# Half of a feed-forward product by seven block products instead of eight, issued as a written stream

## The chip, the cores and the metric

The kernel runs on one core of a Trainium2 chip. The metric is the device time of one execution in microseconds; the time given is the median of several runs, and one execution more is taken with the profiler.

## The reference

One residual block over 256 tokens of width 2048: a retention branch and a latent-attention branch, merged by gates, and then a feed-forward block. The change touches the feed-forward block alone:

```python
def _rmsnorm(x, g):
    x32 = x.astype(jnp.float32)
    y = x32 * lax.rsqrt(jnp.mean(x32 * x32, axis=-1, keepdims=True) + EPS)
    return (y * g.astype(jnp.float32)).astype(x.dtype)

def reference(...):
    h = x
    for l in range(DEPTH):                      # DEPTH = 1
        u = _rmsnorm(h, norm_mix_g[l])
        h = h + _mixer(u, ...)                  # the two branches and w_out
        z = _rmsnorm(h, norm_mlp_g[l]) @ w_up[l]          # (256, 2048) @ (2048, 8192)
        h = h + jnp.square(jax.nn.relu(z)) @ w_down[l]    # (256, 8192) @ (8192, 2048)
    return _rmsnorm(h, norm_f_g)
```

All data is float32.

## The kernel before

**Arithmetic.** Each float32 operand is split in two parts of the type fp32r: `hi` is a cast on ScalarE, `lo` is the rest, by a subtraction on VectorE (`split`, line 214, and `weights`, line 146, which also loads the weight tile with a DMA from SP's queue). A product then takes three matmuls: hi by hi, hi by lo and lo by hi. Activations are kept as `Pair` tiles, whose hi and lo lie side by side for each block of 128 channels, channels on partitions and tokens along the free axis.

**Units.** `t_unit` (line 170) makes one tile of 128 output columns for all 256 tokens: the stationary operand is a 128x128 block of weights. `t_pass1` (line 157) runs w_hi against x_hi and x_lo together, 16 matmuls of 512 columns; `t_pass2` (line 162) runs w_lo against x_hi, 16 of 256. The two halves of the PSUM tile `z` are then added (`join`, line 204: a copy on ScalarE and a sum on VectorE). Weights come in half units of 512 KB. `n_tile` (line 196) is the other form: blocks of x are stationary, 512 columns of weights move, and the result has tokens on partitions.

**Feed-forward.** After the output projection (four column chunks `c`, tile `wo`, from line 770), `mlp_turn` (line 757) transposes the normalized rows on TensorE and splits them into `hT`. The first feed-forward product is the loop over `FT` = 64 units (lines 792 to 800), each followed by a squared ReLU on VectorE into `hid`, which stays in SBUF. The second product (lines 819 to 832) goes over the 64 blocks of `hid`: each is split into `dh` and `dl`, and `down` (line 807) runs 24 matmuls of 512 columns into eight PSUM tiles `dn`, which take all eight banks. The end (`finish`, `normalize`) scales, adds the residual `hn` and normalizes.

**Order.** The program is written in loops; a scheduler with a modelled timeline fixes each engine's order and the slots of the tiles. Engines work through their own lists in order and wait for each other through semaphores. Where the order matters, single instructions are marked `keep_in_program_order`. Tiles come from pools: `wp` holds weights (5 raw, 4 hi, 4 lo tiles of 4 KB a partition), `act` six large tiles, `pmm` and `pat` four PSUM banks each. Only ScalarE and VectorE evict PSUM; GpSimd works on the position angles at the start (lines 296 to 304), on a few small powers, and on the final gain (line 847).

Of the kernel before, what the change touches and what calls it, by code (L numbers as in the profile page):

```python
# [27 lines left out]
CHUNK = 64  # L28
DFF = 8192
FT = DFF // P  # L30
EPS = 1e-6
QK_SCALE = float(192.0 ** -0.5)
LOWEST = -3.4e38
# [55 lines left out]
def block_kernel(ctx: ExitStack, tc: tile.TileContext, A):  # L89
    nc = tc.nc  # L90
    V, SC, G, PE = nc.vector, nc.scalar, nc.gpsimd, nc.tensor
# [3 lines left out]
    cp = ctx.enter_context(tc.tile_pool(name="cp", bufs=1))  # L95
# [4 lines left out]
    def big(name, dt=F32, shape=(P, KT, S)):  # L100
        return act.tile(list(shape), dt, tag="act16", name=name)
# [31 lines left out]
    def mmps(name):  # L133
        return pmm.tile([P, 512], F32, tag="mm", name=name)
# [4 lines left out]
    uid = [0]  # L139
# [15 lines left out]
    HK = KT // 2  # L155
# [40 lines left out]
    def n_tile(out, w, x, t, k0, nk, start, stop):  # L196
# [4 lines left out]
        for k in range(nk):  # L201
            PE.matmul(out, x.hi(k0 + k, ts), w[1][:, k], start=False, stop=stop and k == nk - 1)

    def join(out, ps):
        t = sm.tile([P, S], F32, tag="join", bufs=2, name="join")
        SC.copy(t, ps[:, S:])
        V.tensor_tensor(out=out, in0=ps[:, :S], in1=t, op=ALU.add)  # L207

    def joined(ps):
        t = sm.tile([P, S], F32, tag="val", bufs=2, name="val")  # L210
        join(t, ps)
        return t

    def split(hi, lo, val, scale=None):
        if scale is None:
            SC.copy(hi, val)  # L216
            V.tensor_tensor(out=lo, in0=val, in1=hi.bitcast(F32), op=ALU.subtract)
# [12 lines left out]
    warm = cp.tile([P, 1], F32, name="warm")  # L230
    SC.activation(warm, halfpi, AF.Copy)

    cold = cp.tile([P, 512], BF16, name="cold")
# [5 lines left out]
    rctx = ExitStack()  # L239
    rope_pool = rctx.enter_context(tc.tile_pool(name="rope", bufs=2))  # L240
    ictx = ExitStack()
    ip = ictx.enter_context(tc.tile_pool(name="ip", bufs=1))

# [8 lines left out]
    x = Pair("x")  # L252
# [97 lines left out]
    rxb = cp.tile([P, S], F32, name="rxb")  # L350
    V.tensor_copy(rxb, pb[:, :S])

    tabs = []
# [1 line left out]
    def table(j):  # L355
        ang, kk = angs[j]
        sgn = vec[:, V_INV + 2 + j : V_INV + 3 + j]
        own = ip if j == 0 else cp
        cos = own.tile([P, S], F32, name=f"cos{j}")
        sin = own.tile([P, S], F32, name=f"sin{j}")  # L360
# [157 lines left out]

    with ExitStack() as mctx:
        cc = big("cc", F32R, shape=(P, 2 * LT, 2, S))  # L520
        kpe = cp.tile([P, S], F32, name="kpe")
        lp = ExitStack()
        lpool = lp.enter_context(tc.tile_pool(name="lp", bufs=1))

# [230 lines left out]
    hT = Pair("hT")  # L755

    def mlp_turn(c):
        for jj in range(2):
            pT = atps(f"ht{c}{jj}")
            for j in range(2):  # L760
                kt = 4 * c + 2 * jj + j
                for t in range(2):
                    o = j * S + t * P
                    PE.transpose(pT[:, o : o + P], hn[:, t, kt * P : (kt + 1) * P], ident)
                g = vec[:, V_MLP + kt : V_MLP + kt + 1]
                split(hT.hi(kt), hT.lo(kt), pT[:, j * S : (j + 1) * S], scale=g)
    hp = ctx.enter_context(tc.tile_pool(name="hp", bufs=1))
    ssh = cp.tile([P, 2, 4], F32, name="ssh")
# [22 lines left out]
    hid.append(hp.tile([P, KT, S], F32, name="hid3"))  # L791
    for i in range(FT):
        if i < 2:
            pz = up[i]
            t_half(pz, A["w_up"][i], hT, 1)
        else:
            pz = mmps(f"z{i}")
# [5 lines left out]
    ssf = cp.tile([P, 2, 68], F32, name="ssf")  # L803
    rf = cp.tile([P, 2], F32, name="rf")
    LAST = 2

    def down(i, t, c, w, hs):
        (hi, lo), (dh, dl) = w, hs
        ts = slice(t * P, (t + 1) * P)
        ws = slice(c % 2 * 512, c % 2 * 512 + 512)  # L810
        out = pd[t][c]
        end = i == FT - 1
        mm = tc.keep_in_program_order if i >= FT - LAST else (lambda ins: ins)
        mm(PE.matmul(out, dh[:, ts], hi[:, ws], start=i == 0, stop=False))  # L814
        mm(PE.matmul(out, dh[:, ts], lo[:, ws], start=False, stop=False))  # L815
        mm(PE.matmul(out, dl[:, ts], hi[:, ws], start=False, stop=end))  # L816

    tail = []
    for i in range(FT):
        dh = hp.tile([P, S], F32R, tag="dh", bufs=3, name=f"dh{i}")  # L820
        dl = hp.tile([P, S], F32R, tag="dl", bufs=3, name=f"dl{i}")
        split(dh, dl, hid[i // KT][:, i % KT])
        ws = []
        for half in range(2):
            w = weights(A["w_down"][i][:, half * 1024 : (half + 1) * 1024], [P, 1024])
            ws.append(w)
            if i < FT - LAST:
                for t in range(2):
                    for c in (2 * half, 2 * half + 1):
                        down(i, t, c, w, (dh, dl))  # L830
        if i >= FT - LAST:
            tail.append((i, ws, (dh, dl)))
# [7 lines left out]
    def finish(t, c, lo, hi, n):  # L840
        h = hn[:, t, c * 512 + lo : c * 512 + hi]
        ps = pd[t][c][:, lo:hi]
        V.scalar_tensor_tensor(h, in0=ps, scalar=rh2[:, t : t + 1], in1=h, op0=ALU.mult, op1=ALU.add)
        junk = hp.tile([P, 512], F32, tag="junk", bufs=2, name=f"junk{t}{n}")
# [32 lines left out]
def _t_units(w):  # L877
    k, n = w.shape
    return np.ascontiguousarray(w.reshape(k // P, P, n // P, P).transpose(2, 1, 0, 3))


def _n_units(w):
    k, n = w.shape
    u = w.reshape(k // 512, 4, P, n // 512, 512).transpose(3, 0, 2, 1, 4)
    return np.ascontiguousarray(u.reshape(-1, P, 4, 512))


def _cols(v):
# [57 lines left out]
```

## Time and profile before

| | |
|---|---|
| median of 3 runs | 1631.68 us (1631.11 to 1632.01) |
| the profiled execution | 1632.22 us, its span 1630.4 us |
| granted TensorE clock | 0.998 |
| first feed-forward product | 915.5 to 1272.7 us from the start |
| second feed-forward product | 1272.7 to 1620.6 us (last matmul's start) |
| weights of 512 KB, issue to landing | 4.2 us median |

The profile is one execution. Its page gives each engine's busy time and the chain of work that ended last, followed back from the end; further views give groups of instructions by line, by tile, in order of time, and the busy time in stretches. In a row of the timeline stand the start in us, the time in us, the engine, the line of the kernel, the operation, the tiles (out<-in), the shape and how many instructions were merged. TensorE's matmuls are pipelined, so the duration of one (0.39 us) is longer than the distance from one to the next.

### The profile page before, as it was taken

Reading aid. Unit: us, or ns where it says so; the run is one execution under the profiler, and the core shown is the slowest. Engines: PE = TensorE matmul, PEld = TensorE weight load, DVE = VectorE, ACT = ScalarE, POOL = GpSimd, SP = SyncE. Lnnn points to the kernel's source line nnn. Section 1 sums busy time; section 2 is a strip of 40 time slices with the busy share of each in tenths; the row PEclk is TensorE's granted clock in tenths of the full one; section 3 lists DMA queues with packets and bytes.
Section 4 is the critical chain, followed back from the end, with each engine's and each line's share of the span. In section 5 each row is a group of like instructions: output and inputs, shape, how many; then the busy total and the mean of one; then the engine's idle time right before and its main releaser. Section 6 shows DMA issues by size and latency. Waiting matters only on the chain.

```text
span 1630.4 us, 23041 instructions
## 1 busy us (share of the span) xinstructions
PE 1614.9 (99%) x8782; PEld 1398.8 (86%) x8782; DVE 996.2 (61%) x1491; ACT 809.7 (50%) x1249; POOL 49.5 (3%) x62
## 2 busy tenths in 40 slices
PE   8999999999999999999999999999999999999997
PEld 6888888888889889888888888888888888888886
DVE  7974588655556658666765555555555555555555
ACT  6544555544445556765545544444444444444444
POOL 7100000000000000000000000000000000000001
PEclk9999999999999999999999999999999999999999
DMA  8665544555556554325575555555555655555553
GB/s 306 200 233 193 187 156 166 169 192 186 190 170 203 190 191 146 125 94 176 186 246 187 174 193 188 192 189 186 191 192 184 223 194 192 193 193 195 192 194 112
DMA packets 84480, 304.46 MB, mean 187 GB/s; under 512 B 9360, under 2 KB 9488, under 8 KB 83600
## 3 DMA queue, kind: packets, MB, share of 16 engines
q1 hardware_dynamic: 84368, 302.98, 55.3%
q8 instruction: 69, 1.13, 0.3%
q14 instruction: 43, 0.35, 0.1%
HBM read 300.84 MB, written 2.10 MB: 186 GB/s over the span
## 4 chain that ended last, share of the span: by engine, by line
PE 97%; DVE 1%; issue 0%; DMA 0%; ACT 0%; POOL 0%; SPq 0%; DVEq 0%; POOLq 0%; ACTq 0%
PE z L159 14%; PE z L163 8%; PE dn L816 7%; PE dn L814 7%; PE dn L815 7%; PE rg L159 4%; PE yr L159 4%; PE gr L159 4%; PE gm L159 4%; PE mo L159 4%; PE qk L159 2%; PE gr L163 2%; PE yr L163 2%; PE gm L163 2%; PE rg L163 2%; PE mo L163 2%
## 5 line engine op out<-in xcount | busy, mean ns | idle before, releaser
L152 DVE TENSOR_TENSOR lo<-raw,hi 128x1024 fp32r<-128x1024 f32 (+2 forms) x562 | 666.0, 1204 | 521.6 <-ACT hi L151 248.3
L151 ACT CAST hi<-raw 128x1024 fp32r<-128x1024 f32 (+2 forms) x562 | 580.8, 1035 | 536.9 <-PE z L159 135.2
L159 PE MATMUL z<-hT,hi 128*128 128x512 f32 x1024 | 245.5, 391 | 0.0
L159 PEld LDWEIGHTS z<-hT,hi 128*128 128x128 f32 x1024 | 188.0, 188 | 36.1
L815 PE MATMUL dn<-lo,dh 128*128 128x512 f32 x512 | 199.2, 389 | 0.0
L816 PE MATMUL dn<-hi,dl 128*128 128x512 f32 x512 | 199.2, 389 | 0.0
L814 PE MATMUL dn<-hi,dh 128*128 128x512 f32 x512 | 198.9, 389 | 0.0
L163 PEld LDWEIGHTS z<-hT,lo 128*128 128x128 f32 x1024 | 131.6, 191 | 5.1
L163 PE MATMUL z<-hT,lo 128*128 128x256 f32 x1024 | 133.1, 283 | 0.0
L815 PEld LDWEIGHTS dn<-lo,dh 128*128 128x128 f32 x512 | 96.1, 188 | 20.1
L816 PEld LDWEIGHTS dn<-hi,dl 128*128 128x128 f32 x512 | 96.1, 188 | 19.9
L814 PEld LDWEIGHTS dn<-hi,dh 128*128 128x128 f32 x512 | 96.1, 188 | 19.8
L216 ACT CAST dh<-hid 128x256 fp32r<-128x256 f32 x64 | 26.0, 407 | 89.3 <-PE dn L815 89.3
L159 PE MATMUL mo<-my,hi 128*128 128x512 f32 x256 | 65.5, 396 | 0.4 <-DVE val L207 0.4
L159 PE MATMUL rg<-x,hi 128*128 128x512 f32 x256 | 64.0, 395 | 0.0
L159 PE MATMUL yr<-ry,hi 128*128 128x512 f32 x256 | 61.4, 391 | 0.0
L159 PE MATMUL gr<-x,hi 128*128 128x512 f32 x256 | 61.3, 391 | 0.0
L159 PE MATMUL gm<-x,hi 128*128 128x512 f32 x256 | 61.1, 391 | 0.0
L159 PEld LDWEIGHTS gm<-x,hi 128*128 128x128 f32 x256 | 47.0, 188 | 9.1
L159 PEld LDWEIGHTS gr<-x,hi 128*128 128x128 f32 x256 | 47.0, 188 | 9.0
L159 PEld LDWEIGHTS yr<-ry,hi 128*128 128x128 f32 x256 | 46.9, 188 | 9.0
L159 PEld LDWEIGHTS rg<-x,hi 128*128 128x128 f32 x256 | 46.2, 188 | 8.6
(271 smaller groups left out, 2239.1 us busy)
## 6 DMA issues: line engine op xcount, KB each, us to landing
raw<-w_up SPq DMA_DIRECT2D x128, 512.0 KB, 4.2
raw<-w_down SPq DMA_DIRECT2D x128, 512.0 KB, 4.3
raw<-w_rv SPq DMA_DIRECT2D x32, 512.0 KB, 4.5
raw<-w_rg SPq DMA_DIRECT2D x32, 512.0 KB, 4.5
raw<-w_gret SPq DMA_DIRECT2D x32, 512.0 KB, 4.3
raw<-w_ret_o SPq DMA_DIRECT2D x32, 512.0 KB, 4.6
raw<-w_gmla SPq DMA_DIRECT2D x32, 512.0 KB, 4.4
raw<-w_out SPq DMA_DIRECT2D x32, 512.0 KB, 3.7
```

The costliest lines, as they stand in the source:

```text
L151: SC.copy(hi, raw)
L152: V.tensor_tensor(out=lo, in0=raw, in1=hi.bitcast(F32), op=ALU.subtract)
L159: PE.matmul(out, w[0][:, k], x.both(k0 + k), start=start and k == 0, stop=False)
L163: PE.matmul(out[:, :S], w[1][:, k], x.hi(k0 + k), start=False, stop=stop and k == n - 1)
L216: SC.copy(hi, val)
L814: mm(PE.matmul(out, dh[:, ts], hi[:, ws], start=i == 0, stop=False))
L815: mm(PE.matmul(out, dh[:, ts], lo[:, ws], start=False, stop=False))
L816: mm(PE.matmul(out, dl[:, ts], hi[:, ws], start=False, stop=end))
```

## The change

The weights of the first feed-forward product are divided. The first 4096 columns are computed in 4 passes (`u`) of 1024 columns, each of 8 steps (`j`) of 256 input channels. A step takes x as 2x2 blocks (128 channels by 128 tokens) and w as 2x2 blocks (128 channels by 512 columns) and adds seven block products to seven PSUM tiles, where the plain form has eight. Four of the seven use sums of weight blocks, which are made for every step: two blocks on GpSimd (`fa`), two on VectorE (`fb`). The sums of x blocks (`Combos.make`) are made once, on VectorE. At the end of a pass `s_end` combines the seven tiles to four result blocks, in part on GpSimd; they have tokens on partitions and are transposed on TensorE (`turn`). The other 4096 columns are computed in 32 plain units (`Unit`), in halves.

Steps (four weight parts each) and units (two parts each) are put in one list, three units at the front, two at the back, and mostly one unit behind each step. A loop under `manual_schedule` issues, for each part, the loads seven parts ahead, the splits four ahead, then the part's matmuls; all five engines keep this order. The halves of a unit are added on GpSimd. The squared ReLU moves to ScalarE (Relu, Square). `hid` is written to DRAM from SP's queue and read back in the second product by GpSimd's queue, two blocks at a time, the plain units' blocks first. `hn` is parked in DRAM meanwhile. Some small tiles move to a pool that closes earlier. (`evict` below is a method of `Unit`.)

```diff
+SU = 4
+SJ = KT // 2
+ST = SU * 1024 // P
+EARLY, LATE = 3, 2
+AHEAD = 4
+PAIRED = 6
+MAKE = 1, 2 * EARLY + 18
+SUMS = (4, 7, 10), (0, 1, 2)
...
+    PRODUCTS = ((3, 0, 0), (4, 0, 1), (2, 1, 0), (5, 1, 1), (6, 2, 0), (1, 2, 1), (7, 3, 0))
+
+    class Combos:
...
+        def make(self, c):
+            if c % 2 == 0:
+                self.t.append(big(f"{self.name}{c // 2}", F32R, (P, KT // 4, 2, 4, P)))
+            x, q = wtile("raw", [P, 2, 2, 2, P]), wtile("raw", [P, 2, 4, P])
+            hi, lo = self.pair.span(4 * c, 4)
+            xs = x.rearrange("p j k t n -> p (j k) (t n)")
+            V.tensor_tensor(out=xs, in0=hi.bitcast(F32), in1=lo.bitcast(F32), op=ALU.add)
...
+            V.tensor_tensor(out=a2, in0=a11, in1=a12, op=ALU.subtract)
+            V.tensor_tensor(out=a5, in0=a11, in1=a21, op=ALU.subtract)
+            yield
+            V.tensor_tensor(out=a6, in0=a2, in1=a21, op=ALU.subtract)
+            V.tensor_tensor(out=a4, in0=a6, in1=a22, op=ALU.add)
+            yield
+            o = self.t[-1][:, c % 2 * 2 : c % 2 * 2 + 2]
+            split(o[:, :, 0], o[:, :, 1], q)
...
+    class Step:
...
+        def load(self, part):
+            if part:
+                return
+            self.rb = wtile("raw", [P, 2, 512])
+            self.ra = zp.tile([P, 2, 512], F32, tag="sraw", bufs=2, name=f"sraw{uid[0]}")
+            nc.sync.dma_start(self.ra, self.src[:, :2])
+            nc.sync.dma_start(self.rb, self.src[:, 2:])
+            self.fa, self.fb = (forms[:, 2 * (self.j % 2) + i] for i in range(2))
+            G.tensor_tensor(
+                out=self.fa, in0=self.rb[:, 1:].to_broadcast([P, 2, 512]), in1=self.ra, op=ALU.add
+            )
+
+        def prep(self, part):
+            r = (self.ra, self.fa, self.fb, self.rb[:, :1])[part]
...
+            split(hi, lo, r)
+            self.ws[part] = hi, lo
+            if part == 0:
+                V.tensor_tensor(out=self.fb[:, 0], in0=self.fa[:, 0], in1=self.ra[:, 1], op=ALU.add)
+                V.tensor_tensor(out=self.fb[:, 1], in0=self.fb[:, 0], in1=self.rb[:, 0], op=ALU.add)
+
+        def mm(self, part):
...
+            if part == 1:
+                self.between()
+            hi, lo = self.ws.pop(part)
+            first, last = self.j == 0, self.j == SJ - 1
+            for f, i, o in PRODUCTS:
+                if i == part:
+                    ah, al = self.x.get(f, self.j)
+                    q = self.qs[f]
+                    PE.matmul(q, ah, hi[:, o], start=first, stop=False)
+                    PE.matmul(q, al, hi[:, o], start=False, stop=False)
+                    PE.matmul(q, ah, lo[:, o], start=False, stop=last)
+            if part == 3 and last:
+                self.end()
+
+    def s_end(qs, out, tmp):
...
+        SC.copy(t3, qs[3])
+        tt(V, e, qs[6], t3)
+        SC.copy(q5, qs[5])
+        tt(V, f, qs[2], e, ALU.subtract)
+        SC.copy(c12, qs[1])
+        tt(V, c21, qs[4], f)
+        SC.copy(c22, qs[7])
+        tt(G, c11, q5, f)
+        yield
+        tt(G, e, e, q5, ALU.subtract)
+        yield
+        tt(G, c12, c12, e)
+        yield
+        tt(G, c22, c22, t3)
+        yield
...
+        if c in (1, 2):
+            for _ in hc.make(c - 1):
+                pass
...
-    up = [mmps(f"z{i}") for i in range(2)]
-    for i in range(2):
-        t_half(up[i], A["w_up"][i], hT, 0)
-        if i == 0:
-            mlp_turn(3)
-    hid = [big(f"hid{i}") for i in range(3)]
...
-            t_unit(pz, A["w_up"][i], hT)
-        z = joined(pz)
-        V.scalar_tensor_tensor(hid[i // KT][:, i % KT], in0=z, scalar=0.0, in1=z, op0=ALU.max, op1=ALU.mult)
+    hid = [hidd.tile([P, 2, S], F32, name=f"hid{i}") for i in range(FT // 2)]
+    forms = big("forms", shape=(P, 4, 2, 512))
...
+    def store(pair, n, t):
+        SC.activation(t, t, AF.Square)
+        later.append([3, lambda: nc.sync.dma_start(hid[pair][:, n : n + t.shape[1]], t)])
...
+        def evict(self):
+            pair, n = divmod(ST + self.i, 2)
+            t = zp.tile([P, 2, S], F32, tag="hs", bufs=4, name=f"hs{pair}{n}")
+            SC.copy(t, self.ps.rearrange("p (j n) -> p j n", j=2))
+            G.tensor_tensor(out=t[:, 0], in0=t[:, 0], in1=t[:, 1], op=ALU.add)
+
+            def rest():
+                SC.activation(t[:, :1], t[:, :1], AF.Relu)
+                store(pair, n, t[:, :1])
+
+            later.append([2, rest])
...
+    with tc.manual_schedule(engines=MANUAL):
+        for n, (it, h) in enumerate(parts):
+            ahead = AHEAD if n else 2
+            while loaded < min(len(parts), n + ahead + 3):
+                parts[loaded][0].load(parts[loaded][1])
+                loaded += 1
+            while prepped < min(len(parts), n + ahead + 1):
+                parts[prepped][0].prep(parts[prepped][1])
+                prepped += 1
+            it.mm(h)
+            if n == 0:
+                mlp_turn(3)
+                keep = hidd.tile([P, 2, D], F32, name="hnkeep")
+                SC.dma_start(keep, hn)
+                zo = big("zo", shape=(P, 2, 4, 512))
+            elif n in MAKE:
+                making = hc.make(2 + MAKE.index(n))
+            if n < 2 * EARLY or n % 2 == 0:
+                next(making, None)
+            for entry in list(later):
+                entry[0] -= 1
+                if entry[0] < 0:
+                    later.remove(entry)
+                    entry[1]()
...
+    hn = big("hn2", shape=(P, 2, D))
+    nc.sync.dma_start(hn, keep)
...
-    for i in range(FT):
+    for n, i in enumerate((*range(ST, FT), *range(ST))):
+        if n % 2 == 0:
+            hl = hp.tile([P, 2, S], F32, tag="hl", bufs=3, name=f"hl{i}")
+            G.dma_start(hl, hid[i // 2])
...
-        split(dh, dl, hid[i // KT][:, i % KT])
+        split(dh, dl, hl[:, i % 2])
```

More of the change, by code (lines that the diff above doesn't have):

```diff
@@ L30 @@
 FT = DFF // P
+SU = 4
[6 more added lines that the diff above has]
+SUMS = (4, 7, 10), (0, 1, 2)
+MANUAL = {getattr(mybir.EngineType, n) for n in ('Activation', 'DVE', 'PE', 'SP', 'Pool')}
+SSF = 68
 EPS = 1e-6
@@ L202, in n_tile, with __init__, get @@
             PE.matmul(out, x.hi(k0 + k, ts), w[1][:, k], start=False, stop=stop and k == nk - 1)
+    PRODUCTS = ((3, 0, 0), (4, 0, 1), (2, 1, 0), (5, 1, 1), (6, 2, 0), (1, 2, 1), (7, 3, 0))
+    class Combos:
+        FORM = {2: 0, 5: 1, 6: 2, 4: 3}
+        RAW = {1: (1, 0), 3: (0, 1), 7: (1, 1)}
+        def __init__(self, name, pair):
+            self.name, self.pair, self.t = name, pair, []
+        def make(self, c):
[5 more added lines that the diff above has]
+            V.tensor_tensor(out=xs, in0=hi.bitcast(F32), in1=lo.bitcast(F32), op=ALU.add)
+            a11, a12, a21, a22 = (x[:, :, k, t] for t in range(2) for k in range(2))
+            a2, a5, a6, a4 = (q[:, :, f] for f in range(4))
+            yield
[7 more added lines that the diff above has]
+            split(o[:, :, 0], o[:, :, 1], q)
+        def get(self, f, j):
+            if f in self.RAW:
+                k, t = self.RAW[f]
+                ts = slice(t * P, (t + 1) * P)
+                return self.pair.hi(2 * j + k, ts), self.pair.lo(2 * j + k, ts)
+            o = self.t[j // 4][:, j % 4]
+            return o[:, 0, self.FORM[f]], o[:, 1, self.FORM[f]]
@@ new lines, in block_kernel, with __init__ @@
+    class Step:
+        def __init__(self, qs, src, x, j, between, end):
+            self.qs, self.src, self.x, self.j, self.between, self.end = qs, src, x, j, between, end
+            self.ws = {}
+        def load(self, part):
[11 more added lines that the diff above has]
+            r = (self.ra, self.fa, self.fb, self.rb[:, :1])[part]
+            if part:
+                n = r.shape[1]
+                hi, lo = (
+                    zp.tile([P, n, 512], F32R, tag=f"{kind}{n}", bufs=3 * n - 2, name=f"{kind}{uid[0]}{part}")
+                    for kind in ("shi", "slo")
+                )
+            else:
+                hi, lo = (wtile(kind, [P, 2, 512]) for kind in ("hi", "lo"))
+            split(hi, lo, r)
[4 more added lines that the diff above has]
+        def mm(self, part):
+            if part == 0 and self.j == 0:
+                self.qs.update({f: (mmps if f in (3, 4, 2, 5) else atps)(f"zs{uid[0]}{f}") for f in (3, 4, 2, 5, 6, 1, 7)})
+            if part == 1:
[11 more added lines that the diff above has]
+                self.end()
@@ new lines, in s_end, with tt @@
+    def s_end(qs, out, tmp):
+        t3, e, f, q5 = (tmp[:, i] for i in range(4))
+        c11, c12, c21, c22 = (out[:, t, c] for t in range(2) for c in range(2))
+        def tt(eng, o, a, b, op=ALU.add):
+            eng.tensor_tensor(out=o, in0=a, in1=b, op=op)
+        SC.copy(t3, qs[3])
[12 more added lines that the diff above has]
+        tt(G, c22, c22, t3)
+        yield
@@ L231, in block_kernel @@
     SC.activation(warm, halfpi, AF.Copy)
[L233 removed]
+    rctx = ExitStack()
+    rope_pool = rctx.enter_context(tc.tile_pool(name="rope", bufs=2))
+    cold = rope_pool.tile([P, 512], BF16, tag="cold", bufs=1, name="cold")
     V.memset(cold, 0.0)
@@ L357, in table @@
         sgn = vec[:, V_INV + 2 + j : V_INV + 3 + j]
-        own = ip if j == 0 else cp
-        cos = own.tile([P, S], F32, name=f"cos{j}")
-        sin = own.tile([P, S], F32, name=f"sin{j}")
+        cos, sin = (
+            (ip if j == 0 else rope_pool).tile([P, S], F32, tag=f"{name}{j}", bufs=1, name=f"{name}{j}")
+            for name in ("cos", "sin")
+        )
         tc.keep_in_program_order(SC.activation(sin, ang, AF.Sin, scale=sgn))
@@ L764, in mlp_turn @@
                     PE.transpose(pT[:, o : o + P], hn[:, t, kt * P : (kt + 1) * P], ident)
+            for j in range(2):
+                kt = 4 * c + 2 * jj + j
                 g = vec[:, V_MLP + kt : V_MLP + kt + 1]
@@ L767, in block_kernel @@
     hp = ctx.enter_context(tc.tile_pool(name="hp", bufs=1))
+    zctx = ExitStack()
+    zp = zctx.enter_context(tc.tile_pool(name="zp", bufs=1))
+    hidd = ctx.enter_context(tc.tile_pool(name="hidd", bufs=1, space=bass.MemoryType.DRAM))
+    hc = Combos("hc", hT)
     ssh = cp.tile([P, 2, 4], F32, name="ssh")
@@ new lines, in block_kernel, with square, __init__, load @@
+    forms = big("forms", shape=(P, 4, 2, 512))
+    later = []
+    def store(pair, n, t):
+        SC.activation(t, t, AF.Square)
+        later.append([3, lambda: nc.sync.dma_start(hid[pair][:, n : n + t.shape[1]], t)])
+    def square(pair, ps):
+        t = zp.tile([P, 2, S], F32, tag="hs", bufs=4, name=f"hs{pair}")
+        SC.activation(t, ps.rearrange("p (j n) -> p j n", j=2), AF.Relu)
+        store(pair, 0, t)
+    class Unit:
+        def __init__(self, i, order, between=None):
+            self.i, self.order, self.between, self.raw, self.ws = i, order, between, {}, {}
+        def load(self, part):
+            self.raw[part] = wtile("raw", [P, HK, P])
+            nc.sync.dma_start(self.raw[part], A["w_up"][self.i][:, part * HK : (part + 1) * HK])
+        def prep(self, part):
+            hi, lo = (wtile(kind, [P, HK, P]) for kind in ("hi", "lo"))
+            split(hi, lo, self.raw.pop(part))
+            self.ws[part] = hi, lo
+        def mm(self, part):
+            if part == 0:
+                self.ps = atps(f"z{self.i}")
+            w = self.ws.pop(part)
+            t_pass1(self.ps, w, hT, part * HK, HK, part == 0)
+            t_pass2(self.ps, w, hT, part * HK, HK, part == 1)
+            if part:
+                self.evict()
+            if self.between:
+                self.between(part)
+        def evict(self):
[7 more added lines that the diff above has]
+            later.append([2, rest])
@@ new lines, in block_kernel, with turn, step, end @@
+    turns = []
+    def turn(u, jj):
+        pT = atps(f"zt{u}{jj}")
+        for j in range(2):
+            kt = 2 * jj + j
+            for t in range(2):
+                o = j * S + t * P
+                src = zo[:, 0, 2 * t + kt // 4, kt % 4 * P : kt % 4 * P + P]
+                PE.transpose(pT[:, o : o + P], src, ident)
+        square(4 * u + jj, pT)
+    def step(u, j, qs):
+        def end():
+            sums = s_end(qs, zo[:, 0].rearrange("p (t c) n -> p t c n", t=2), zo[:, 1])
+            next(sums)
+            later.extend([d, lambda: next(sums)] for d in SUMS[u == SU - 1])
+            turns.extend(lambda jj=jj: turn(u, jj) for jj in range(4))
+        def between():
+            if turns and j:
+                turns.pop(0)()
+        return Step(qs, A["w_up_s"][u, j], hc, j, between, end)
@@ new lines, in drain, with fn @@
+    def drain(n):
+        def fn(part):
+            for _ in range(n[part]):
+                turns.pop(0)()
+        return fn
+    early = [Unit(i, 0) for i in range(EARLY)]
+    parts = [(e, h) for h in range(2) for e in early]
+    units = iter(range(EARLY, FT - ST - LATE))
+    for u in range(SU):
+        qs = {}
+        for j in range(SJ):
+            st = step(u, j, qs)
+            parts += [(st, h) for h in range(4)]
+            if j != PAIRED and (u, j) != (SU - 1, SJ - 1):
+                un = Unit(next(units), 0)
+                parts += [(un, 0), (un, 1)]
@@ new lines, in block_kernel @@
+    for n, i in enumerate(range(FT - ST - LATE, FT - ST)):
+        un = Unit(i, 0, drain(((0, 1), (1, 2))[n]))
+        parts += [(un, 0), (un, 1)]
+    loaded = prepped = 0
+    making = iter(())
+    with tc.manual_schedule(engines=MANUAL):
[22 more added lines that the diff above has]
+                    entry[1]()
+        while later:
+            later.pop(0)[1]()
@@ L885, in _n_units, with _s_steps @@
     return np.ascontiguousarray(u.reshape(-1, P, 4, 512))
+def _s_steps(w):
+    k, n = w.shape
+    b = w.reshape(k // 256, 2, P, n // 1024, 2, 512)
+    q = np.stack([b[:, 0, :, :, 1], b[:, 1, :, :, 0], b[:, 1, :, :, 1], b[:, 0, :, :, 0]], axis=3)
+    return np.ascontiguousarray(q.transpose(2, 0, 1, 3, 4))
 def _cols(v):
```

32 lines of the change are left out of this document (13 added, 19 removed).

## The prediction

> **What bounds the kernel now.** I read the page first: its engine shares and its chain of waits.
>
> ```profile
> PE 1614.9 (99%) x8782; PEld 1398.8 (86%) x8782; DVE 996.2 (61%) x1491; ACT 809.7 (50%) x1249; POOL 49.5 (3%) x62
> ...
> PE 97%; DVE 1%; issue 0%; DMA 0%; ACT 0%; POOL 0%; SPq 0%; DVEq 0%; POOLq 0%; ACTq 0%
> ```
>
> The chain is TensorE for 97% of the span, so only fewer TensorE microseconds, or a new stall of TensorE, move the time. Next the busy times by stretch: the first feed-forward product (935 to 1270), the crossing to the second (1272 to 1284), the second.
>
> ```profile
> core 0: us, PE busy (x) PEld busy (x) DVE busy (x) ACT busy (x) POOL busy (x), PEclk, DMA share, GB/s
> 935.00:1270.00 335.00, 335.00 (x1926) 296.02 (x1925) 189.95 (x247) 150.00 (x183) 0.00 (x0) 1.00 0.57 190
> 1272.00:1284.00 12.00, 12.00 (x57) 10.05 (x57) 7.11 (x9) 4.30 (x7) 0.00 (x0) 1.00 0.76 247
> 1284.00:1610.00 326.00, 326.00 (x1440) 269.93 (x1439) 172.51 (x180) 144.51 (x179) 0.00 (x0) 1.00 0.57 190
> ```
>
> TensorE never pauses, the clock is full, VectorE is busy 57% and GpSimd not at all. Then the starts of the two products' matmuls, by tile, and the timeline of TensorE where a transpose pair lies among matmuls:
>
> ```profile
> L159 PE MATMUL z<-hT,hi x1024: 389/389/477, 915.5 to 1270.5; 128*128 128x512 f32 x171
> L814 PE MATMUL dn<-hi,dh x512: 389/389/396, 1272.7 to 1620.2; 128*128 128x512 f32 x171
> L816 PE MATMUL dn<-hi,dl x512: 388/389/389, 1273.1 to 1620.6; 128*128 128x512 f32 x171
> ```
>
> ```profile
> 925.05 0.71 PE L159 MATMUL z<-hT,hi 128*128 128x512 f32 x2
> 925.60 0.38 PE L764 MATMUL ht<-con,hn 128*128 128x128 f32 x2
> 925.74 1.64 PE L159 MATMUL z<-hT,hi 128*128 128x512 f32 x6
> ```
>
> Last, the timeline of VectorE and GpSimd near the start, the one place where both work:
>
> ```profile
> 26.21 0.74 POOL L304 TENSOR_TENSOR ang<-ang,step 128x256 f32<-128x256 f32 x1
> 26.27 1.83 DVE L217 TENSOR_TENSOR lo<-lead,hi 128x256 fp32r<-128x256 f32 x3
> 27.04 0.90 POOL L303 TENSOR_SCALAR step<-kk 128x256 f32<-128x256 f32 x1
> 28.03 2.89 DVE L152 TENSOR_TENSOR lo<-raw,hi 128x1024 fp32r<-128x1024 f32 x2
> 28.03 1.81 POOL L304 TENSOR_TENSOR ang<-ang,step 128x256 f32<-128x256 f32 x1
> ...
> 47.45 2.34 DVE L152 TENSOR_TENSOR lo<-raw,hi 128x1024 fp32r<-128x1024 f32 x2
> 49.71 0.41 DVE L207 TENSOR_TENSOR early<-first,join 128x256 f32<-128x256 f32 x1
> ```
>
> Two subtractions of 1024 take 2.34 us alone and 2.89 us when one GpSimd sum of 256 falls among them; that sum takes 1.81 us instead of 0.74. They wait for each other, and VectorE lost 0.55 us. This decides my forecast.
>
> **Prices on TensorE.** The second product starts 1536 matmuls of 512 columns within 347.9 us (1272.7 to 1620.6): 0.2266 us each. The first product lasts from 915.5 to the first `dn` matmul at 1272.7, 357.2 us with 8 transposes in it. Two matmuls and two transposes fill 925.05 to 925.74: (0.69 - 0.45) / 2 = 0.118 us a transpose. So a unit costs (357.2 - 0.9) / 64 = 5.57 us.
>
> **What TensorE gains.** 32 units go: 32 x 5.57 = 178.2 us. 32 steps come, each 7 products of 3 matmuls of 512: 672 x 0.2266 = 152.3 us. Their results lie with tokens on partitions, so 16 turns of 4 transposes are added: 64 x 0.118 = 7.5 us. Net -18.4 us. The other 32 units keep their matmuls, only in halves. In the output projection two `make` calls add some 3.6 us of VectorE each (two passes of 1024, four of 256) to a 22 us column chunk of which eight subtractions take some 10: TensorE covers it; uncovered it would be 7 us.
>
> **What VectorE and GpSimd are given.** Back-to-back pitch is the row's duration less about 0.08 (2.34 for two of 1.21): 1.13 for 1024, 0.61 for 512 (rows of 0.69), 0.34 for 256 (0.42). A step gives VectorE subtractions of 1024, 1024, 1024 and 512 and two sums of 512: 3 x 1.13 + 3 x 0.61 = 5.22 us, for 4.76 us of matmuls. A unit gives it 2.26 us for 5.57 us. The end of a pass adds three PSUM sums, 1.8 us.
>
> GpSimd gets one sum of 1024 a step, one of 256 a unit, four of 512 a pass. The row of 256 runs alone in 0.74 us and cost VectorE 0.55. The 512 row (the final gain, L847) has a median of 1302 ns, 0.56 us above that of 256, so I take 1.11 us of hold for 512 and 2.2 us for 1024. No row of 1024 exists. The low end is the cost of a one-input GpSimd operation: the three subtractions of 256 at 26.27 took 1.83 us where three alone take 1.10; 0.55 of the 0.73 lost goes to the sum at 26.21, 0.18 to the scalar operation at 27.04. Four times that is 0.7 us for 1024. The high end is the whole duration, 0.74 + 3 x 0.56 = 2.42 us. I take 2.2, since both rows with two inputs give it.
>
> Per pass of eight steps and seven units: TensorE 38.1 + 39.0 + 1.9 = 79.0 us; VectorE 41.8 + 15.8 + 1.8 = 59.4 us; GpSimd's holds 8 x 2.2 + 7 x 0.55 + 4 x 1.11 = 25.9 us. VectorE's own work fits. With the holds it is 85.3 us: VectorE, held by GpSimd, becomes the bound. Nearly every VectorE operation here reads two SBUF tiles, as the subtractions of the rows do, so there is little for GpSimd to slip under.
>
> The stall over the whole stretch: `AHEAD` lets VectorE finish about the first step while the early units run. After it come 31 steps x 7.42 = 230.0, 27 units x 2.81 = 75.9, the three early units' sums 1.7, three pass ends x 6.2 = 18.7, one `make` 3.6: 329.9 us, starting 1.7 us in (an eviction copy and a cast of 1.05 come first on ScalarE), then the last 0.7 us of matmuls: 332.3 us. TensorE alone needs 152.3 + 27 x 5.57 + 12 turns x 0.47 = 308.3 us. Stall 24.0 us. The last pass end hides under the two late units, 11.1 us.
>
> ScalarE: casts 8 x (3 x 1.05 + 0.62) + 7 x 2.1, unit evictions 7 x 1.4, turns 4 x 1.2, four copies of 0.6 make some 62 us of a 79 us pass, so it follows. Its eviction copy waits for TensorE with four parts of casts already done ahead of it; queued behind it is the next cast, 0.6 us later. SP's stores wait for ScalarE, with weight loads queued behind them, but loads are issued seven parts ahead (some 11 us) against 4.2 us to landing: nothing, and 1 us a store if that lead were gone. Traffic per pair of step and unit is 2 MB of weights and 0.25 MB of stores in 10.4 us, 225 GB/s, under the 247 that the crossing shows.
>
> **The crossing.** `hid` now comes back from DRAM through GpSimd's queue, behind its last sum: copy 0.6, sum 0.74, 256 KB landing 2.5 (the row of `out`), cast 0.41: 4.3 us. Lower end 0, if the load is placed earlier, as the 12.00 of 12.00 above; upper end 8.7, if the `w_down` loads stand behind the last stores on SP (copy, sum, two passes of 0.41, load 4.3, cast 1.05, subtraction 1.13). Later reads have three buffers of two tiles each, some 30 us: hidden; 2.5 us each otherwise. The parked `hn` (2 MB out and back) needs 8.8 us each way by the row `hn<-x`, off the path.
>
> **Sum**, against the profiled execution's 1632.22 us (span 1630.4): -178.2 + 152.3 + 7.5 + 24.0 + 4.3 = +9.9, so 1642.1. The median of the runs is 0.5 lower: 1641.6 us.
>
> **Rivals.**
> *TensorE stays the bound* (faster). If the sums of 1024 held VectorE like the one-input operation, a pass would be 59.4 + 8 us, under 79. It flips where the holds fall below 79.0 - 59.4 = 19.6 us a pass, 1.4 us a sum of 1024; each tenth off the holds is 10 us off the stall. Then only the crossing is left: 1632.2 - 18.4 + 4.3 - 0.5 = 1617.6, or 1613.3 without it. For it: VectorE alone fits, and the holds are measured at 256 only. Against: both rows scale with size. 0.25.
> *Holds partly covered.* GpSimd can run ahead by a step, and some sums fall where VectorE waits at a pass end or for a cast. Half of the stall gone: 1629.6. 0.1.
> *GpSimd holds for its whole duration* (slower still). 0.19 us more for each of some 73 sums: +13.9, 1655.5. The rows speak against it: 0.55 lost of 0.74. 0.08. The Trainium skill, "SBUF — State Buffer", section "Who interferes with whom", has this as its rule: VectorE with two SBUF inputs and a GpSimd instruction that reads SBUF lock each other out, the second waiting until the first is finished; the 0.55 of 0.74 agrees with the waiting, not quite with the length.
> My forecast has 0.57.
>
> **Chances.** A measurement of this kernel can tell a change of about 0.2%, 3.3 us, from none. Faster: the first rival and a quarter of the second, 0.28. Same: most of the second, 0.08. Slower: 0.64. The forecast's own range is 1631 to 1650 (holds a tenth lower, or half way to the whole duration); to leave out no more than 2 in 10 it must reach into the first rival: 1615 to 1652.
>
> **What would show it.** Right: in the step stretch VectorE is busy over 90%, TensorE about 93% with its idle time ended by the `lo` subtractions; VectorE subtractions of 1024 average well over 1.3 us; GpSimd's busy time rises to about 170 us or more. Wrong: TensorE 98% there and subtractions at 1.22 us, which is the first rival; or a gap over 10 us at the first `dn` matmul.

## The result, and the profile after

The changed kernel takes 1649.26 us (median of 4 runs, 1649.00 to 1649.51) against 1631.85 us before: a ratio of 1.0108, 95% interval 1.0090 to 1.0125. It is slower, as forecast, and within the range, 0.7 us under the upper end of the forecast's own (1631 to 1650); the size was 17.4 us where 9.9 were forecast. The profiled execution took 1649.21 us, its span is 1647.4 us.

From the page, the lines that answer to those of before:

```profile
PE 1608.8 (98%) x8494; PEld 1373.9 (83%) x8494; DVE 1160.5 (70%) x1527; ACT 894.9 (54%) x1397; POOL 217.6 (13%) x174
...
PE 81%; DVE 9%; issue 4%; DMA 2%; POOL 2%; ACT 2%; SPq 0%; DVEq 0%; POOLq 0%; ACTq 0%
```

VectorE stands in the chain with 9% where it had 1%, and TensorE has lost 16 points. The busy times by stretch show where: the second and third pass (by their first matmul), the crossing, the second product.

```profile
core 0: us, PE busy (x) PEld busy (x) DVE busy (x) ACT busy (x) POOL busy (x), PEclk, DMA share, GB/s
1022.50:1109.20 86.70, 81.45 (x411) 68.15 (x410) 85.14 (x66) 56.54 (x79) 37.67 (x20) 0.98 0.61 205
1109.20:1196.10 86.90, 81.39 (x409) 68.21 (x409) 85.39 (x66) 56.34 (x79) 37.43 (x20) 0.98 0.60 205
...
1273.00:1291.00 18.00, 17.78 (x101) 15.35 (x102) 16.01 (x14) 13.96 (x21) 9.91 (x6) 1.00 0.85 292
1291.00:1610.00 319.00, 319.00 (x1410) 264.16 (x1409) 167.74 (x175) 144.59 (x183) 15.74 (x29) 1.00 0.69 220
```

VectorE is busy 85.1 and 85.4 us of a pass of 86.7 and 86.9: it is the bound. What the prediction named as signs of being right is there: TensorE is busy 94% of these passes, and of its 23.8 us of waits from the first unit to the second product 16.2 end with a `lo` subtraction; another 7.0 end with an eviction copy of ScalarE. VectorE's busy time holds waiting inside instructions. In the groups of the first product by shape, the mean (second number behind the bar) of one and the same kind of subtraction, 128x1024, differs by what lies beside it:

```profile
L336 DVE TENSOR_TENSOR lo<-raw,hi 128x1024 fp32r<-128x1024 f32 x62 | 132.8, 2179 | 7.1 <-ACT hi L335 7.1
L263 POOL TENSOR_TENSOR forms<-raw,sraw 128x1024 f32<-128x1024 f32 x32 | 92.3, 2889 | 409.3 <-DMA raw<-w_up_s 408.2 <-DVE slo L336 1.1
L336 DVE TENSOR_TENSOR slo<-forms,shi 128x1024 fp32r<-128x1024 f32 x64 | 79.6, 1252 | 0.0
```

Units' subtractions (`lo<-raw`) take 2179 ns where they took 1222 before; those of the weight sums (`slo<-forms`), which mostly meet no GpSimd work, take 1252. One such meeting in order of time, VectorE and GpSimd first, then TensorE in the same microseconds:

```profile
1093.22 1.21 DVE L336 TENSOR_TENSOR lo<-sraw,hi 128x1024 fp32r<-128x1024 f32 x1
1093.84 2.85 POOL L263 TENSOR_TENSOR forms<-raw,sraw 128x1024 f32<-128x1024 f32 x1 [1.09 <-DMA raw<-w_up_s]
1094.36 2.88 DVE L280 TENSOR_TENSOR forms<-forms,sraw 128x512 f32<-128x512 f32 x1
1097.27 0.69 DVE L281 TENSOR_TENSOR forms<-forms,raw 128x512 f32<-128x512 f32 x1
```

```profile
1095.74 0.40 PE L295 MATMUL zs<-shi,hc 128*128 128x512 f32 x1
1099.15 0.80 PE L296 MATMUL zs<-slo,hc 128*128 128x512 f32 x1 [3.01 <-DVE slo L336]
1099.74 0.63 PE L294 MATMUL zs<-shi,hc 128*128 128x512 f32 x1
1100.17 0.63 PE L295 MATMUL zs<-shi,hc 128*128 128x512 f32 x1
```

A VectorE sum of 512 that takes 0.68 us elsewhere (the second sum of the step, at 1097.27, takes 0.69) takes 2.88 us, because GpSimd's sum of 1024 got in at 1093.84: 2.20 us of hold, the price of the prediction. TensorE, at the end of its run ahead, waits for the subtraction behind it: its next matmul starts 3.4 us after the last one, 3.0 us of them idle. Then it runs at half clock: starts 0.43 us apart instead of 0.227.

### The profile page after: what moved, and what is told of

It is laid out like the page before. It is cut to its first block, busy times and chain, and to the rows that moved or that the text cites. A ratio compares the mean times of both kernels' runs of the same rounds, so it can differ in the third digit from the quotient of the medians.

```text
span 1647.4 us, 22896 instructions
## 1 busy us (share of the span) xinstructions
PE 1608.8 (98%) x8494; PEld 1373.9 (83%) x8494; DVE 1160.5 (70%) x1527; ACT 894.9 (54%) x1397; POOL 217.6 (13%) x174
## 4 chain that ended last, share of the span: by engine, by line
PE 81%; DVE 9%; issue 4%; DMA 2%; POOL 2%; ACT 2%; SPq 0%; DVEq 0%; POOLq 0%; ACTq 0%
PE dn L1057 7%; PE dn L1056 7%; PE dn L1055 7%; DVE lo L336 4%; PE rg L169 4%; PE yr L169 4%; PE gr L169 4%; PE gm L169 4%; PE mo L169 4%; PE qk L169 2%; PE z L169 2%; DVE slo L336 2%; PE gr L173 2%; PE yr L173 2%; PE gm L173 2%
## 5 line engine op out<-in xcount | busy, mean ns | idle before, releaser
L162 DVE TENSOR_TENSOR lo<-raw,hi 128x1024 fp32r<-128x1024 f32 (+2 forms) x434 | 517.5, 1206 | 366.2 <-ACT hi L161 231.4
L161 ACT CAST hi<-raw 128x1024 fp32r<-128x1024 f32 (+2 forms) x434 | 446.1, 1030 | 390.6 <-PE dn L1057 96.8
L263 POOL TENSOR_TENSOR forms<-raw,sraw 128x1024 f32<-128x1024 f32 x32 | 92.3, 2889 | 409.3 <-DMA raw<-w_up_s 408.2
L336 DVE TENSOR_TENSOR lo<-raw,hi 128x1024 fp32r<-128x1024 f32 x64 | 135.3, 2149 | 10.1 <-ACT hi L335 10.1
L169 PE MATMUL z<-hT,hi 128*128 128x512 f32 x512 | 128.1, 392 | 0.2 <-ACT hs L925 0.2
L335 ACT CAST shi<-forms 128x1024 fp32r<-128x1024 f32 x64 | 67.2, 1050 | 110.2 <-DVE forms L281 101.6
L169 PEld LDWEIGHTS z<-hT,hi 128*128 128x128 f32 x512 | 94.1, 189 | 18.9 <-ACT hs L925 0.6
L336 DVE TENSOR_TENSOR slo<-forms,shi 128x1024 fp32r<-128x1024 f32 x64 | 79.6, 1252 | 0.0
L173 PEld LDWEIGHTS z<-hT,lo 128*128 128x128 f32 x512 | 69.4, 190 | 9.7 <-DVE lo L336 5.1
L335 ACT CAST hi<-raw 128x1024 fp32r<-128x1024 f32 x64 | 64.3, 1049 | 7.2 <-PE wo L210 5.0
```

Of the source, the lines that this page charges most:

```text
L161: SC.copy(hi, raw)
L162: V.tensor_tensor(out=lo, in0=raw, in1=hi.bitcast(F32), op=ALU.subtract)
L169: PE.matmul(out, w[0][:, k], x.both(k0 + k), start=start and k == 0, stop=False)
L173: PE.matmul(out[:, :S], w[1][:, k], x.hi(k0 + k), start=False, stop=stop and k == n - 1)
L263: G.tensor_tensor(out=self.fa, in0=self.rb[:, 1:].to_broadcast([P, 2, 512]), in1=self.ra, op=ALU.add)
```

## The experiments

The time of the kernel before in the four groups of runs was 1631.4 to 1631.7 us; ratios are against it. "Pass" is the mean length of the second and third pass by their first matmuls, as above; the changed kernel's is 86.8 us. Three theories stood against each other. A: VectorE and GpSimd hold each other off, and the sum of VectorE's own work and GpSimd's holds is the bound. B: VectorE's own added work is the bound, GpSimd has no part in it. C: it is a matter of order; the two steps of a pass that stand side by side use up the splits that were made ahead, whichever engine makes the sums.

**Without the sum of 1024.** The first two blocks stand in for their sum.

```diff
-            G.tensor_tensor(
-                out=self.fa, in0=self.rb[:, 1:].to_broadcast([P, 2, 512]), in1=self.ra, op=ALU.add
-            )
+            (self.fa is self.ra)
```

> The sum of 1024 on GpSimd is left out and its place is taken by the raw blocks themselves, so that part of the computation is missing; everything else, VectorE's work among it, is as in the changed kernel. Theory A: a pass needs 59.4 + 8.3 = 67.7 us of VectorE with holds, TensorE's 79.0 is the bound: 1613 to 1619 us. Rival B: VectorE's own work is unchanged, so the time is too, 1645 to 1650 us. Rival C: over 1640 us.

Measured: 1617.08 us, ratio 0.991 (0.989 to 0.9929). TensorE is the bound again; VectorE's own work is what it was:

```profile
1011.40:1091.00 79.60, 79.30 (x410) 67.44 (x409) 66.79 (x66) 56.55 (x79) 12.89 (x12) 1.00 0.66 223
1091.00:1170.60 79.60, 79.30 (x411) 67.44 (x409) 66.78 (x66) 56.55 (x79) 12.95 (x12) 1.00 0.65 223
```

The same 66 instructions of VectorE take 66.8 us a pass here and took 85.1 with the sum. 32 instructions of an engine that was busy 43% of the time cost 32 us of the whole. Rivals B and C fall: VectorE's subtractions, the steps side by side and the order are all still there. With the sum its result goes too, for which others could have had to wait; but in the changed kernel ScalarE's casts waited 8.4 us for it and VectorE's sums 2.3 in the whole product, too little for 32.

**With it twice.**

```diff
             G.tensor_tensor(out=self.fa, ...)
+            G.tensor_tensor(out=self.fa, ...)
```

> The sum of 1024 is made twice on GpSimd, the same output both times. Theory A: 32 more holds of 2.2 us on an engine pair that is already the bound: 1649 + 70 = 1719 us, within 10. Rival B: GpSimd is busy 24 of 86 us a pass and has room for 32 x 2.4 us, the time stays within 10 us of 1649. Rival C: the same as rival B.

Measured: 1717.04 us, 67.8 more than with one, or 2.1 us a sum. The pass is 104.1 us, VectorE busy 103.3 of it:

```profile
1041.20:1144.50 103.30, 86.28 (x411) 70.16 (x410) 101.94 (x66) 56.64 (x79) 61.31 (x27) 0.95 0.51 172
1144.50:1249.40 104.90, 86.82 (x410) 70.27 (x409) 104.56 (x66) 56.73 (x79) 62.27 (x28) 0.93 0.49 169
```

In the changed kernel GpSimd had 49 us a pass free, and the second sum still went into the time in full.

**One input instead of two.** A copy in the place of the sum.

```diff
-            G.tensor_tensor(out=self.fa, in0=..., in1=self.ra, op=ALU.add)
+            G.tensor_copy(self.fa, self.ra)
```

> GpSimd's sum of 1024 is replaced by a copy of 1024, one input for two; the sum itself is left out. Theory A with the price of the prediction's low end: a copy holds VectorE by 0.7 us, a pass needs 59.4 + 8.3 + 5.6 = 73.3 us, TensorE is the bound: 1614 to 1620 us, and the longest subtraction of 1024 that meets a copy takes 1.9 to 2.0 us. Rival (any GpSimd instruction on 1024 holds for 2.2 us, whatever its inputs): 1645 to 1653 us.

Measured: 1624.36 us, ratio 0.9955 (0.9938 to 0.9971), 4 us over the expected range, far from the rival's. The timeline of VectorE and GpSimd where a copy falls on two subtractions that alone take 2.34 us together:

```profile
1047.80 1.04 POOL L263 COPY forms<-sraw 128x1024 f32<-128x1024 f32 x1
1048.02 3.03 DVE L334 TENSOR_TENSOR lo<-raw,hi 128x1024 fp32r<-128x1024 f32 x2 [1.53 <-ACT hi L333]
```

The hold is 0.69 us, and 0.7 was the low end that the prediction took from a scalar operation of 256. Subtractions that meet a copy alone take 1.90 us, as expected; the longest of all take 2.3. VectorE is busy 72.9 us a pass (73.3 by the sum), the pass takes 81.2. So the bound was lifted, but a gap of some 2.2 us a pass stayed, in which TensorE's transposes wait for an eviction copy (`hs`, on ScalarE).

**Only the sum of 1024 left on GpSimd.**

```diff
-            G.tensor_tensor(out=t[:, 0], in0=t[:, 0], in1=t[:, 1], op=ALU.add)
+            V.tensor_tensor(out=t[:, 0], in0=t[:, 0], in1=t[:, 1], op=ALU.add)
...
-        tt(G, c11, q5, f)                  (and the three others of s_end)
+        tt(V, c11, q5, f)
```

> Only the sum of 1024 stays on GpSimd, made ahead as in the changed kernel; the units' sums of 256 and the pass end's of 512 go to VectorE. Theory A (holds and own work add up): own 59.4 + 2.4 + 2.4 = 64.2, holds 17.6, together 81.8 us a pass instead of 85.3: 14 us less than 1649, so 1632 to 1638 us. Rival (the small sums fall where VectorE waits anyway, and only the sum of 1024 costs): 1.2 us more work a pass for VectorE, 1649 to 1654 us.

Measured: 1640.08 us, ratio 1.0056 (1.0038 to 1.0074): 9 us less, where theory A said 11 to 17 and the rival 0 to 5 more. VectorE is busy 82.9 us a pass, 81.8 by the sum, but the pass takes 84.2: full, and still with gaps of 2.6 to 3.3 us at the two steps that stand side by side.

**The pair of steps elsewhere.**

```diff
-PAIRED = 6
+PAIRED = 3
```

> The unit that is missing between two steps is missing behind step 3 instead of step 6; work and engines are unchanged. Theory A: the sum of a pass is the same, 85.3 us, so the time stays within 4 us of 1649; the long gaps move with the pair, and half clock with them. Rival C (the two steps side by side just ahead of the pass end are the cause): the gaps of 3.4 us go and with them the stretches at half clock, 10 us or more, under 1640 us.

Measured: 1649.02 us, ratio 1.0107 (1.0091 to 1.0123): no change, as theory A has it. The gaps of 3.4 us did break up, none of the new ones is over 2.7, but more of them came, and three stretches at half clock stayed. Where the bursts stand decides how the loss is cut up, not how much it is.

**The sum of 1024 on VectorE**, behind the step's first subtraction; then **all sums on VectorE** (this edit and that of the fourth run together).

```diff
-            G.tensor_tensor(out=self.fa, ...)          (in load)
...
             if part == 0:                              (in prep, behind the split)
+                V.tensor_tensor(out=self.fa, ...)
                 V.tensor_tensor(out=self.fb[:, 0], in0=self.fa[:, 0], in1=self.ra[:, 1], op=ALU.add)
```

> Theory A (VectorE and GpSimd hold each other off, the sum of both is the bound): the sum of 1024 costs VectorE 1.13 us itself instead of a hold of 2.2, so a pass needs 59.4 + 9.0 + 8.3 = 76.7 us of VectorE with holds, under TensorE's 79.0. Of the 35.7 us in which TensorE stood or ran at half clock from the first unit to the last down matmul, at most 12 stay: 1614 to 1626 us. Rival B (VectorE's own added work, subtractions and sums, is the bound, not GpSimd): 9 us more a pass, 1649 + 36 = 1685 us. Rival C (the two steps of a pass that stand side by side drain the splits ahead, whoever sums): the gaps of 3.4 us stay and the time is over 1640 us.

> All sums of the stretch on VectorE, none on GpSimd. Theory A: VectorE's own work is 59.4 + 9.0 + 2.4 + 2.4 = 73.2 us a pass against TensorE's 79.0, no holds are left: 1614 to 1622 us, subtractions of 1024 at 1.22 us. Rival B: 13.8 us more a pass, 1649 + 55 = 1704 us. Rival C: over 1640 us, as the steps side by side stay.

Measured: 1644.25 us, ratio 1.0076 (1.0061 to 1.0091), and 1631.48 us, ratio 0.9999 (0.9990 to 1.0009). Better than with GpSimd by 5 and 18 us, but theory A promised 1614 to 1626. B's 1685 and 1704 are farther off. The first time lies where C put it, over 1640, but without C's gaps: behind the pair of steps the longest gap left is 1.2 us, and a gap of 3.1 us in each of the last three passes, in which TensorE waits for an eviction copy on ScalarE, has come instead.

Some 6 us of either time have a cause that no theory had. The first casts of the second product (`dh`) stand early in ScalarE's order, in the first pass, and wait 5.0 and 4.6 us for the read-back of `hid`. The next cast of a step comes late, TensorE's matmuls start 4.35 and 3.93 us apart there, and half clock adds some 2 us. In the second run:

```profile
948.33 0.71 ACT L335 CAST dh<-hl 128x256 fp32r<-128x256 f32 x2 [4.58 <-DMA hl<-hid]
950.04 0.79 PE L294 MATMUL zs<-shi,hc 128*128 128x512 f32 x1 [3.53 <-ACT shi L335]
```

By this estimate the first time would lie under 1640 without it. In the second run's passes VectorE is full no more:

```profile
1017.60:1099.30 81.70, 80.38 (x410) 67.06 (x409) 76.00 (x85) 56.81 (x80) 0.00 (x0) 1.00 0.64 217
```

The two longest waits of these passes, between 1010 and 1180 us (engine and line, whom it waited for: us in total, times, longest):

```profile
ACT shi L335 <- DVE forms L277: 45.0, 17, 3.3
DVE lo L336 <- ACT hi L335: 9.5, 10, 1.3
```

Made on GpSimd, the sum ran ahead of its step. On VectorE it stands between the step's splits: ScalarE cannot cast the sum before VectorE has made it (2.6 us each time), its next casts come late, and VectorE waits for those. The two engines take turns. Adding up each engine's work does not show that; theory A2 below names it.

**The three weight sums two parts earlier**, still all on VectorE, in the issuing loop:

```diff
             while prepped < min(len(parts), n + ahead + 1):
+                soon = parts[prepped + 2] if prepped + 2 < len(parts) else (None, 1)
+                if soon[1] == 0 and isinstance(soon[0], Step):
+                    soon[0].sums()          (fa and both fb, no longer in prep)
                 parts[prepped][0].prep(parts[prepped][1])
```

> All sums on VectorE as in the second run (1631.5 us), but a step's three sums of weights stand two parts earlier in VectorE's order. Theory A2 (the second run was not bound by VectorE's work, busy 76.0 of 81.7 us a pass, but by turns: ScalarE waits 2.8 us a step for the sum, and VectorE then for ScalarE's next casts): the wait goes, a pass takes 79.6 us as without the sum, 1615 to 1622 us. Rival B2 (VectorE is simply too full, with 93% of TensorE's time): no change, 1629 to 1634 us.

Measured: 1636.32 us, ratio 1.0028 (1.0018 to 1.0039): a miss for both, and slower than without the move. By pass the answer is split:

```profile
932.60:1023.00 90.40, 81.62 (x395) 67.80 (x394) 79.53 (x93) 56.64 (x81) 2.44 (x4) 0.96 0.63 212
1023.00:1103.60 80.60, 79.98 (x410) 67.09 (x409) 74.50 (x84) 56.22 (x79) 0.00 (x0) 1.00 0.64 218
```

The middle passes came down from 81.7 to 80.6 us; the first, which took 85.6 in the second run, went up to 90.4. VectorE's timeline in it:

```profile
987.00 1.23 DVE L265 TENSOR_TENSOR forms<-raw,sraw 128x1024 f32<-128x1024 f32 x1 [3.96 <-DMA raw<-w_up_s]
```

VectorE stood 3.96 us for a load. The sum now comes before its weights; while a `make` is at work it holds two of the five raw tiles, and the loads wait for them.

**One part earlier, two parts earlier, and a longer run ahead**, each with the last `make` working in `zo`, which is empty then, instead of two raw tiles.

```diff
-                x, q = wtile("raw", ...), wtile("raw", ...)
+                x, q = z[:, 0, :2], z[:, 0, 2:]       (z is zo; the shapes as before)
...
-                soon = parts[prepped + 2] ...         (first and third of the group)
+                soon = parts[prepped + 1] ...
...
-AHEAD = 4                                             (third of the group)
+AHEAD = 5
```

> All sums on VectorE, a step's three weight sums one part earlier than in the second run, and the last sums of x blocks made in the tile that waits for the pass end, so that they take no raw weight tiles. Theory A2: with two parts earlier the middle passes took 80.6 us, and what was lost stood in the first and last pass (gaps of 4.5 and 3.6 us), where VectorE's sum came ahead of its load; with one part the load has landed: passes near 80 us throughout, 1618 to 1625 us, faster than the kernel before. Rival B2 (VectorE too full): 1630 us or more.

> The same, but two parts earlier, as in the run of 1636.3 us; against that run only the raw tiles are freed. Theory A2: the gap of 4.5 us in the first pass, which stood behind a load that waited for a raw tile, goes, the one in the last pass may stay: 1624 to 1632 us. Rival: the load is late for another reason, 1634 to 1638 us.

> As the first of this group, with splits five parts ahead and loads eight instead of four and seven. Theory A2: VectorE and ScalarE have 5 to 6 us a pass to spare and a longer run ahead takes up bursts: equal to the first of this group or up to 4 us faster. Rival (a longer run ahead meets the limits of the weight tiles, 5 raw and 4 hi): slower by 2 us or more.

Measured: 1621.55 us, ratio 0.9940 (0.9927 to 0.9952); 1631.86, ratio 1.0000 (0.9992 to 1.0009); 1619.23, ratio 0.9921 (0.9908 to 0.9935). All three lie where A2 put them, the second at the edge. With the sums two parts earlier, freeing the raw tiles is worth 4.5 us; one part instead of two is worth 10.3, the longer run ahead 2.3. No run moves the sums one part ahead without freeing the raw tiles; but in the second and third pass no `make` is at work, and there the first run of this group takes 79.6 us where the run with all sums on VectorE took 81.7, so that much is the move alone. In the third run VectorE fits beside TensorE, and the clock is full; its second pass, which holds a gap of 1.5 us, and its third:

```profile
1012.50:1093.00 80.50, 79.37 (x409) 67.26 (x409) 76.81 (x87) 58.23 (x81) 0.00 (x0) 1.00 0.70 227
1093.00:1172.20 79.20, 79.20 (x411) 67.60 (x410) 75.29 (x85) 57.05 (x79) 0.00 (x0) 1.00 0.67 224
```

Nothing is left out in this kernel, and it beats both: 12 us under the kernel before and 30 under the changed one.

**The same run ahead, with GpSimd.** The changed kernel with `AHEAD = 5` and `make` in `zo`, its sums left where they were.

> The changed kernel with its sums on GpSimd as they are, but with the longer run ahead (five and eight parts) and the last sums of x blocks out of the raw tiles, as in the fastest run. Theory A (the sum of own work and holds, 85.3 us a pass, is the bound): a longer run ahead cannot help by more than the half clock and the bursts, 1642 to 1649 us. Rival C (bursts and order, not the sum, cost the time): 1630 us or less.

Measured: 1661.21 us, ratio 1.0182 (1.0165 to 1.0199): 12 us slower still, which neither theory expected. So a longer run ahead is no gain by itself. Its second pass, and three of its longer waits between 1010 and 1190 us:

```profile
1020.80:1110.60 89.80, 81.45 (x410) 68.26 (x409) 79.10 (x66) 56.50 (x80) 40.64 (x19) 0.96 0.59 197
...
POOL forms L267 <- DMA raw<-w_up_s: 54.0, 8, 9.1
ACT shi L339 <- DVE forms L285: 36.9, 15, 6.0
...
DVE lo L340 <- ACT hi L339: 21.9, 10, 3.5
```

VectorE is busy 79.1 us of 89.8, so here own work and holds are not the bound. GpSimd itself waits for weights, and the wait seems to be handed on to VectorE's sums, ScalarE's casts and VectorE's subtractions. In each of the last three passes TensorE's transposes wait for an eviction copy, a gap of 6.5 us with 6.8 us at half clock about its end. Why the loads come late in this order I did not take apart.

## Why the prediction was right

**The mechanism** was the one forecast: VectorE and GpSimd hold each other off, and own work and holds add up to the bound. The run without the sum and the run with two show it from both sides, 32.2 us down and 67.8 us up. The step "GpSimd's holds" came out as priced where one sum meets VectorE alone: 2.20 us for 1024 and, from the meetings of a 512 subtraction with a unit's sum (1.22 to 1.24 us against 0.68), 0.55 for 256. "85.3 us a pass" for VectorE with holds was measured as 85.3 (mean of the two passes); without the sum 66.8 against 67.7, with two 103.3 against 102.9.

**The size** fell short by 7.5 us. From the first unit to the last `dn` matmul's start the span is 722.6 us (914.7 to 1637.3) against 705.1 before. By the prediction's prices TensorE needs 705.1 - 18.4 = 686.7, so 35.9 us were lost where 28.3 were forecast:
- The stall, forecast at 24.0: the distances of over 0.48 us between matmul starts, less 0.23 each, make 27.7 us. Among them are gaps of up to 2.5 us in which TensorE waits for the eviction copy, which stands behind casts that wait for VectorE; the prediction's "so it follows" for ScalarE left them out. VectorE in its turn waits 2.4 us for ScalarE's casts in the second and third pass together. How the difference divides between the two is not shown.
- Half clock, not forecast: three stretches of 3.4 us, each behind a gap of over 3 us, at half speed: some 5 us.
- The crossing, forecast at 4.3: nothing to be seen, TensorE is busy 17.78 of 18.00 us, since the first `dn` matmuls start at 1281.9 among the last units' matmuls. The lower end, 0, was right. The 4.3 us that did not come hid a part of the shortfall: without them 35.9 us stand against 24.0.
- What is left, some 3 us, is gaps below that size.

**The rivals.** "TensorE stays the bound" priced its case at 1617.6 with the crossing or 1613.3 without it; the run without the sum of 1024 took 1617.1. As the crossing cost nothing, 1613.3 is the figure to compare, and that the other agrees is chance. What this rival lacked is the full hold of the sum. "Whole duration" (1655.5) lies even a little nearer to the measured 1649.3 than the forecast's 1641.6, so the time alone does not decide against it. The trace does: a sum lasts at least 2.38 us and holds for 2.20, a copy 1.04 and holds for 0.69. The rule of the Trainium skill, "SBUF — State Buffer", section "Who interferes with whom", is so confirmed as to who waits for whom, and a little too long as to how much.

**What adding up could not say** is what a move of the sums would bring. The first expectations took each engine's work alone, and missed by 18 and 10 us at their upper ends; the order within the step, the wait for `hid` in the first pass and the landing of the weights made the rest.

## What to carry to other kernels

An engine that stands idle is not free if its instructions hold off the one that is full: price GpSimd's elementwise work as time taken from VectorE, by the length of a hold that the trace shows, and here that was dearer (2.2 us) than doing the sum on VectorE (1.13). When each engine's work fits and the time still does not come down, look for two engines that take turns inside one step, and move the first link of that chain ahead, but not ahead of its loads. A gap of some 3 us in TensorE can cost more than itself.

## What the runs showed of the hardware that was not expected

TensorE's clock fell to half for 3.4 us at a time behind gaps of 3.25, 3.41 and 3.40 us (matmul starts 0.43 us apart instead of 0.227), up to 1.7 us each on top of the gap; in the run with two sums nine such stretches lie in the first product, 3.4 or 6.8 us long. The Trainium skill, "TensorE: Matmul & The Clock Gate", Part 1, gives a window of 3413 ns and half rate after an idle one; the traces agree with that length, but not with a whole idle window as the condition, since shorter gaps brought half clock too. Which gap brings it on is not a matter of its size alone: one of 2.30 us did in the run with the pair moved, and one of 3.26 us in the run with only the large sum on GpSimd did not; gaps of 2.2 to 2.5 us brought none in the changed kernel.

Two GpSimd instructions with the same output, 1024 elements a partition, held VectorE for 2.20 us (a sum, two inputs) and 0.69 us (a copy, one input). A sum of 256 held it for 0.55 of its 0.74 us, one of 1024 for 2.20 of 2.38: in both the hold is some 0.2 us shorter than the instruction.
